# Moving the triangle of the decays from GpSimd to VectorE, with other pauses in the mixers and x loaded one tile ahead

## The chip, the cores and the metric

The kernel runs on one core of a Trainium2 chip. The metric is the device time of one launch in microseconds (us), median of three runs. One layer of a streaming encoder is computed for a prompt of 512 frames and a sample of 64.

The engines go by the names of the profile: PE is TensorE's matrix products and PEld its weight loads, DVE is VectorE, ACT is ScalarE, POOL is GpSimd, and SP issues most of the transfers. L187 is line 187 of the kernel before; the changed kernel's lines around the mixers are 2 higher.

## The reference

```python
def trunk(...):
    mod = jax.nn.silu(c) @ w_ada[l] + b_ada[l]
    sh1, sc1, g1, sh2, sc2, g2 = jnp.split(mod[:, None, :], N_MOD, axis=-1)
    h = rmsnorm(x, norm1[l]) * (1 + sc1) + sh1
    mix, s_a, s_b, s_c = token_mixers(h, ...)      # h @ w_in, mixers, @ w_out
    x = x + g1 * mix
    h = rmsnorm(x, norm2[l]) * (1 + sc2) + sh2
    f, s_f = conv_ffn(h, ...)                      # w_up, conv, silu * val, w_down
    x = x + g2 * f
    y = rmsnorm(x, final_norm)

def gdn_step(s, blk):                              # 8 heads, blocks of 64 frames
    q, k, v, g, beta = blk
    big_g = jnp.cumsum(g[..., 0], axis=-1)
    decay = jnp.exp(jnp.where(causal, big_g[..., :, None] - big_g[..., None, :], -jnp.inf))
    lower = jnp.where(strict, einsum('bhid,bhjd->bhij', kb, k) * decay, 0.0)
    sol = solve_triangular(eye + lower, concat([v * beta, kb * exp(big_g)]), unit_diagonal=True)
    u = sol[..., :dv] - einsum('bhik,bhkv->bhiv', sol[..., dv:], s)
    attn = einsum('bhid,bhjd->bhij', q, k) * decay
    o = einsum('bhid,bhdv->bhiv', q * exp(big_g), s) + einsum('bhij,bhjv->bhiv', attn, u)
    s_new = exp(g_last) * s + einsum('bhjd,bhjv->bhdv', k * exp(g_last - big_g), u)
```

Everything is float32. Beside the 8 heads of this delta rule (GDN) there are 4 heads of gated linear attention (GLA), with a decay for each channel. `q` and `k` of GDN are scaled to unit length, and each head's output is normed by its root mean square.

## The kernel before

**Projections.** A weight tile of 8 k-tiles of 128 x 128 is loaded, copied by ACT to a rounded high half `wh` (L629), and the rest is subtracted by DVE to a low half `wl` (L630); three buffers hold each half. A k-tile is six products on TensorE (L542 four times, L544 twice): high by high, high by low, low by high, each for two halves of 288 frames. After every k-tile `gemm` calls `tick`. The time from 150 us to about 1180 us holds w_in's projection and the first half of w_out's.

**Mixers.** `gdn` (9 jobs: 8 heads and one of the samples, which works in blocks of 64) and `gla` are generators. Each tick advances some of them to their next `yield`, so their instructions are written between the k-tiles. `rest(n)` yields n ticks. `self.later(n, f)` runs f after n ticks. The list of instructions of each engine is then made by a scheduler that goes by the order of writing, except that DVE's and ACT's mixer instructions (`jv`, `ja`, class `_Sooner`, all on line L1650 of the profile) are pulled forward by 80 places, and weight loads and splits as well. An engine then runs its list in order. A pause therefore decides where an instruction stands in its engine's list; when it runs is up to the data and to what stands ahead of it.

**A GDN job** goes through these steps, four blocks of 128 frames side by side in tiles of 128 x 512 (`m`):

1. `kF`, `qF` are transposed on TensorE (L145) and squared on ACT; `rsqrt` adds on DVE (L138) and takes the power −1/2 on POOL (L139).
2. Differences of the decays' sums are taken on DVE; POOL's two `affine_select` (L187, L188) set the upper or lower triangle to −200 or +200, so that the exponentials give 0 there. For the samples two POOL memsets (L190, L191) set corners too.
3. ACT scales `kT`, TensorE transposes it (L145, "bank<-consts,m"), ACT takes the exponential of `dl`; then come the products of k by k (L208) and of k by q (L216).
4. `inverse16` inverts the 16 x 16 blocks on the diagonal on POOL: DMA out (L342), loads as 32 lanes (L348), memset (L352), 14 steps of a product and a sum (L358, L359), a copy (L362), DMA out (L363), loads back (L367); DVE spreads the two results (L372). All of this stands on POOL's single list, with POOL's other work of other heads before or behind it.
5. Two levels on TensorE extend the inverse to 64 (L231, L237). Then four state steps, each with `w` copied by ACT (`sq`, half a tile) and used by L283, L299; the outputs `ops` are normed (`rsqrt` on four columns), transposed (L145) and put away.

**w_out and x.** Before each output tile of 8 k-tiles, `x_tile` loads one slice of x (L1117, L1118 on SP), transposes it (L145, "xr") and copies it to its place; `residual` adds the product to it (L1094). In the background DVE multiplies w_ada for the later modulations (L770), throughout the mixers' time.

## Time and profile before

| | us |
|---|---|
| median of 3 runs | 2985.03 (2980.51 to 2990.21) |
| the profiled execution | 2986.52 |
| its span | 2984.7 |
| PE busy | 2893.7 (97%) |
| DVE busy | 2098.1 (70%) |
| ACT busy | 1226.2 (41%) |
| POOL busy | 360.7 (12%) |
| mean granted clock of TensorE | 0.987 |

The span is what the profile shows between the first and the last instruction; 1.8 us of the execution's time lie around it. In a row of the timeline stand the start, the duration, the engine, the line, the operation, what is written and read, and in brackets the idle time ahead of it on its engine with what ended it. TensorE's clock is given as a share of the full speed.

### The profile page before, as it was taken

The page shows a single profiled execution, that of the slowest core. Times are in us where ns is not written, and L with a number is a line of the kernel's source. Part 1 is how long each engine was busy: PE and PEld are TensorE (multiplying, and loading weights), DVE is VectorE, ACT ScalarE, POOL GpSimd, SP SyncE. Part 2 cuts the span into 40 slices and gives each one's busy share as a digit, 9 for nine tenths or more (in the row PEclk, how much of TensorE's full clock was granted, in tenths as well). Part 3 has the DMA queues.
Part 4 walks back from the last instruction along what each step waited for, and adds up shares of the span by engine and source line. Part 5 has one row for each costly group of instructions (what it writes and reads, how often), then busy time and mean ns, then how long its engine had stood idle before and what let it go on. Part 6 is the DMA issues. An engine that isn't in the chain of part 4 may idle for free.

```text
span 2984.7 us, 52378 instructions
## 1 busy us (share of the span) xinstructions
PE 2893.7 (97%) x21128; PEld 2788.1 (93%) x21128; DVE 2098.1 (70%) x3225; ACT 1226.2 (41%) x2116; POOL 360.7 (12%) x634
## 2 busy tenths in 40 slices
PE   7998989999999999999999999999999999999998
PEld 3588989999889998999999999999999999999997
DVE  5776767766569877367888888888888865555555
ACT  6564544544244333255444444444444432212223
POOL 0025433234311001000000000000000000000000
PEclk9999999999999999999999999999999999999999
DMA  7855545554445547443333333333333473333221
GB/s 271 284 165 140 150 132 150 155 143 137 137 125 148 147 136 208 131 129 93 106 104 110 97 107 106 111 97 104 108 110 98 130 236 97 117 102 109 87 85 66
DMA packets 509446, 392.96 MB, mean 132 GB/s; under 512 B 41385, under 2 KB 438404, under 8 KB 509204
## 3 DMA queue, kind: packets, MB, share of 16 engines
q1 hardware_dynamic: 503780, 378.93, 42.8%
q0 software_dynamic: 5424, 10.68, 1.1%
q8 instruction: 167, 2.74, 0.4%
q14 instruction: 75, 0.61, 0.1%
HBM read 355.16 MB, written 34.36 MB: 131 GB/s over the span
## 4 chain that ended last, share of the span: by engine, by line
PE 63%; DVE 2%; DMA 1%; ACT 1%; issue 1%; POOL 0%; SPq 0%; ACTq 0%; POOLq 0%; DVEq 0%
PE g L542 19%; PE g L544 9%; PE g L1324 8%; PE g L1325 8%; PE g L1326 8%; PE bank L1324 3%; PE bank L1325 3%; PE bank L1326 3%; DVE acc L770 1%; PE bank L417 1%; DVE m L1650 0%; DVE wl L630 0%; PE bank L145 0%; PE bank L1534 0%; PE bank L776 0%
## 5 line engine op out<-in xcount | busy, mean ns | idle before, releaser
L542 PE MATMUL g<-slot,wh 128*128 128x288 f32 x3168 | 550.7, 295 | 0.2 <-DVE slot L1094 0.2
L1324 PE MATMUL g<-slot,wh 128*128 128x290 f32 x1760 | 534.0, 303 | 2.0 <-ACT p L1336 1.6
L1325 PE MATMUL g<-slot,wh 128*128 128x290 f32 x1760 | 526.8, 299 | 0.0
L1326 PE MATMUL g<-slot,wl 128*128 128x290 f32 x1760 | 521.1, 296 | 0.0
L629 ACT ACTIVATE wh<-raw 128x1024 fp32r<-128x1024 f32 x223 | 235.9, 1058 | 630.7 <-PE g L542 607.1
L542 PEld LDWEIGHTS g<-slot,wh 128*128 128x128 f32 x3168 | 463.5, 188 | 0.8 <-DVE slot L1094 0.5
L542 PE MATMUL g<-hh,wh 128*128 128x288 f32 x1984 | 458.3, 311 | 1.6 <-DVE gcb L933 1.0
L542 PE MATMUL g<-hl,wh 128*128 128x288 f32 x1984 | 437.4, 300 | 0.5 <-DVE hl L1104 0.5
L544 PE MATMUL g<-hh,wl 128*128 128x288 f32 x1984 | 434.6, 299 | 0.6 <-DVE wl L630 0.6
L1094 DVE SCALAR_TENSOR_TENSOR slot<-g,mod,slot 128x512 f32<-128x512 f32 (+1 forms) x448 | 201.8, 492 | 303.6 <-PE g L544 302.4
L1271 ACT ACTIVATE wh<-raw 128x1024 fp32r<-128x1024 f32 x176 | 186.8, 1061 | 392.6 <-PE g L1325 379.4
L1324 PEld LDWEIGHTS g<-slot,wh 128*128 128x128 f32 x1760 | 331.5, 188 | 16.5 <-ACT p L1336 10.6
L544 PE MATMUL g<-slot,wl 128*128 128x288 f32 x1584 | 341.8, 295 | 0.0
L1326 PEld LDWEIGHTS g<-slot,wl 128*128 128x128 f32 x1760 | 337.0, 191 | 0.0
L1325 PEld LDWEIGHTS g<-slot,wh 128*128 128x128 f32 x1760 | 335.6, 191 | 0.1
L542 PEld LDWEIGHTS g<-hh,wh 128*128 128x128 f32 x1984 | 320.1, 191 | 6.0 <-issue 1.4
L542 PEld LDWEIGHTS g<-hl,wh 128*128 128x128 f32 x1984 | 324.2, 191 | 1.5 <-DVE hl L1104 1.0
L630 DVE TENSOR_TENSOR wl<-raw,wh 128x1024 fp32r<-128x1024 f32 x223 | 272.5, 1222 | 73.8 <-ACT wh L629 71.1
L544 PEld LDWEIGHTS g<-hh,wl 128*128 128x128 f32 x1984 | 322.8, 190 | 1.1 <-DVE wl L630 0.8
L544 PEld LDWEIGHTS g<-slot,wl 128*128 128x128 f32 x1584 | 255.7, 188 | 0.0
L770 DVE SCALAR_TENSOR_TENSOR acc<-xr,ct,acc 128x512 f32<-128x512 f32 x322 | 229.9, 755 | 3.4 <-DMA xr<-in_w_ada_dram 3.4
L1272 DVE TENSOR_TENSOR wl<-raw,wh 128x1024 fp32r<-128x1024 f32 x176 | 214.9, 1221 | 18.6 <-ACT wh L1271 18.5
(373 smaller groups left out, 4571.0 us busy)
## 6 DMA issues: line engine op xcount, KB each, us to landing
raw<-in_w_up_dram SPq DMA_DIRECT2D x176, 512.0 KB
raw<-in_w_in_dram SPq DMA_DIRECT2D x108, 512.0 KB
raw<-in_w_down_dram SPq DMA_DIRECT2D x88, 512.0 KB
xr<-in_w_ada_dram SPq DMA_DIRECT2D x86, 512.0 KB
hraw<-in_w_ada_dram SPq DMA_DIRECT2D x64, 512.0 KB
ax<-in_w_ada_dram SPq DMA_DIRECT2D x42, 512.0 KB
raw<-in_w_out_dram SPq DMA_DIRECT2D x32, 512.0 KB
slot<-actd SPq DMA_DIRECT2D x44, 288.0 KB
```

Of the source, the lines that this page charges most:

```text
L417: T.matmul(ps[:, b * 64:(b + 1) * 64], e3[:, b], qc[:, b * 64:(b + 1) * 64], start=True, stop=True)
L542: T.matmul(ps[:, h if bank is None else bank, :n], wh, x[:, h, :n], start=f, stop=False)
L544: T.matmul(ps[:, h if bank is None else bank, :n], wl, ah[:, h, :n], start=False, stop=stop)
L629: nc.scalar.activation(hi[:, :n_], raw[:, :n_], AF.Copy)
L630: nc.vector.tensor_tensor(lo[:, :n_], raw[:, :n_], hi[:, :n_].bitcast(F32), op=ALU.subtract)
L770: V.scalar_tensor_tensor(acc[s], w[:, k], col, acc[s], op0=ALU.mult, op1=ALU.add)
L1094: self.nc.vector.scalar_tensor_tensor(x1[:, :, z], ps[:, :, c], gain[:, q:q + 1], x1[:, :, z], op0=ALU.mult, op1=ALU.add)
L1271: self.nc.scalar.activation(hi, src, AF.Copy)
L1272: self.nc.vector.tensor_tensor(lo, src, hi.bitcast(F32), op=ALU.subtract)
L1324: T.matmul(ps, wh[:, j], hi, start=(c < 3 and j == 0), stop=False, skip_group_check=True)
L1325: T.matmul(ps, wh[:, j], lo, start=False, stop=False, skip_group_check=True)
L1326: T.matmul(ps, wl[:, j], hi, start=False, stop=(j == NPAIR - 1), skip_group_check=True)
```

## The change

- A new constant `far` (128 more columns of constants) holds 200 above the diagonal and 0 elsewhere. On DVE one instruction takes the minimum of `dl` and `far` − 200, another the maximum of `dl` and `far`; POOL's two `affine_select` of each job are gone. The two memsets of the samples stay on POOL. One of five `sq` buffers makes room.
- The pause ahead of the memsets and of `kT` is REST_L = 9 instead of REST_T = 6, and stands behind the triangle.
- Each of the 14 steps of the inverse is followed by 2 ticks (1 or 2 before), REST_P is 2 for 6, 2 ticks come between the copy and the DMA, and REST_X is 12 for 16.
- REST_G, the pause of GLA's levels, is 4 for 3; `turn`, the transposes of GLA's `v`, is put off by 8 ticks instead of 3.
- x's slice is loaded while the output tile before is worked on, and transposed behind its own tile's products.

```diff
--- before.py
+++ after.py
@@ -32,10 +32,11 @@
 JOB_RATE, ADA_RATE = 1.0, 0.65
 
 
-REST_D, REST_X, REST_T, REST_N, REST_G = 8, 16, 6, 8, 3
+REST_D, REST_X, REST_T, REST_N, REST_G = 8, 12, 6, 8, 4
 REST_C = 14
-HOP, REST_P, REST_S = 3, 6, 4
+HOP, REST_P, REST_S = 3, 2, 4
 PUT, PUT_O = 24, 6
+REST_L = 9
 MOST = 2
 FAR = 200.0
 LATE = 3
@@ -77,6 +78,7 @@
     for s in LEVELS:
         m[f"p{s}"] = _pair_mask(s)
     m["bd16"] = (r[:, None] // 16 == r[None, :] // 16) * 1.0
+    m["far"] = up * FAR
     m["tri"] = up * 1.0
     m["tri2"] = (up & bd) * 1.0
     m["l127"] = np.repeat((r == 127)[:, None], P, 1) * 1.0
@@ -130,7 +132,7 @@
         return self.sp.tile([P, w], F32, tag=f"s{w}", bufs=6, name=self.name(f"s{w}"))
 
     def half(self):
-        return self.sp.tile([P, P], F32, tag="sq", bufs=5, name=self.name("sq"))
+        return self.sp.tile([P, P], F32, tag="sq", bufs=4, name=self.name("sq"))
 
 
     def rsqrt(self, out, src, n, parts=P):
@@ -183,9 +185,9 @@
         self.rsqrt(rr, ss, 8)
         dl, du = self.m4(), self.m4()
         V.tensor_tensor(dl, gb, self.col4(gcol), op=ALU.subtract)
-        yield from self.rest(REST_T)
-        nc.gpsimd.affine_select(du, dl, pattern=[[0, 4], [1, P]], compare_op=ALU.is_ge, fill=-FAR, base=0, channel_multiplier=-1)
-        nc.gpsimd.affine_select(dl, dl, pattern=[[0, 4], [-1, P]], compare_op=ALU.is_gt, fill=FAR, base=0, channel_multiplier=1)
+        V.scalar_tensor_tensor(du, self.bc4(c["far"]), -FAR, dl, op0=ALU.add, op1=ALU.min)
+        V.tensor_tensor(dl, dl, self.bc4(c["far"]), op=ALU.max)
+        yield from self.rest(REST_L)
         if pair:
             nc.gpsimd.memset(du[0:64, :, 64:P], -FAR)
             nc.gpsimd.memset(dl[64:P, :, 0:64], FAR)
@@ -351,8 +353,7 @@
             self.ja.activation(kT[:, b], kT[:, b], AF.Copy, scale=wk[:, b:b + 1])
         G.memset(lane[:, 0, 0:256:17], 1.0)
         for i in range(1, 15):
-            if i % 2:
-                yield WAIT
+            yield WAIT
             rest = slice(i + 1, 16)
             sh = [32, 15 - i, i]
             G.tensor_tensor(xt[:, rest, :i], xx[:, rest, i:i + 1].to_broadcast(sh), xx[:, i:i + 1, :i].to_broadcast(sh), op=ALU.mult)
@@ -360,6 +361,7 @@
             yield WAIT
         yield from self.rest(REST_P)
         G.tensor_copy(xt, xx.rearrange("p i j -> p j i"))
+        yield from self.rest(2)
         G.dma_start(d1.rearrange("w q f -> q w f"), lane)
         yield from self.rest(REST_S)
         cm = self.sp.tile([P, 2, 4, 16], F32, tag="cm", bufs=2, name=self.name("cm"))
@@ -1074,7 +1076,7 @@
                     if f == 1:
                         x["v"] = lambda: [vT[b // 2][:, b % 2] for b in range(4)]
 
-                self.later(HOP, turn)
+                self.later(REST_T + 2, turn)
             if h == 3:
                 xs["v"] = self.gla_sample_v
             for f in range(2):
@@ -1108,14 +1110,18 @@
         return lambda k0, k1: (self.i[name][0, (k_off + k0) * P:(k_off + k1) * P, m * P:(m + 1) * P]
                                .rearrange("(k p) n -> p k n", p=P))
 
-    def x_tile(self, m):
-
-        nc, i = self.nc, self.i
-        t = self.slot(self.x_place(m), F32)
-        raw = self.xr()
+    def x_load(self, m):
+
+        nc, i, raw = self.nc, self.i, self.xr()
         n = slice(m * P, (m + 1) * P)
         nc.sync.dma_start(raw[:, :512].rearrange("p (b t) -> p b t", b=4), i["x_prompt"][0, :, n].rearrange("(b p) n -> p b n", p=P))
         nc.sync.dma_start(raw[:TS, 512:512 + P], i["x_sample"][0, :, n])
+        return raw
+
+    def x_tile(self, m, raw):
+
+        nc = self.nc
+        t = self.slot(self.x_place(m), F32)
         nc.gpsimd.memset(t[:, :, HP:ZS], 0.0)
         ps = self.transpose4(raw[:, :512].rearrange("p (b t) -> p b t", b=4))
         nc.scalar.activation(t[:, :, :HP], ps.rearrange("p (h b) t -> p h (b t)", h=2), AF.Copy)
@@ -1599,10 +1605,13 @@
                     K.run_later(all=True)
                     ob = [K.load_o(k, lambda k=k: K.htiles(k)) for k in range(8, 16)]
                     K.x1 = []
+                    raw = K.x_load(0)
                     for m in range(KD):
                         ps = K.pgt()
-                        K.x1.append(K.x_tile(m))
                         K.gemm(ps, K.w_cols("w_out", m, 8), ob, tick=K.tick)
+                        nxt = K.x_load(m + 1) if m + 1 < KD else None
+                        K.x1.append(K.x_tile(m, raw))
+                        raw = nxt
                         K.residual(ps, K.x1[m], K.mod[:, 2, m])
                     K.drain()
                     for _ in K.ada:
```

How the order of the instructions moves is shown at three places. The first is ACT's list where head 4's differences (m_727 and m_728 before, m_734 and m_735 now) stand near head 2's first `w` (sq_676), the copy that TensorE's L283 reads. Before:

```order
L1650 ACT_TABLE_LOAD
L1650 ACTIVATE m_711_4474<-m_711_4474 128x512
L1650 ACTIVATE m_647_4042<-bank_673_4294,beta_1586 128x128 x4
L1650 ACTIVATE m_727_4625<-m_727_4625 128x512
L1650 ACTIVATE m_728_4626<-m_728_4626 128x512
L1650 ACTIVATE sq_676_4331<-bank_675_4329 128x128
L1650 ACTIVATE m_727_4625<-m_727_4625,nbeta_1608 128x128 x3
L1650 ACTIVATE m_647_4042<-bank_679_4344,rq_466_2817 128x128
```

And in the change:

```order
L1659 ACTIVATE m_644_4023<-bank_674_4283,beta_1586 128x128 x4
L1659 ACT_TABLE_LOAD
L1659 ACTIVATE m_711_4452<-m_711_4452 128x512
L1659 ACTIVATE sq_676_4318<-bank_675_4316 128x128
L1659 ACTIVATE m_734_4633<-m_734_4633 128x512
L1659 ACTIVATE m_735_4634<-m_735_4634 128x512
L1659 ACTIVATE m_644_4023<-bank_679_4330,rq_463_2792 128x128
L1659 ACTIVATE m_734_4633<-m_734_4633,nbeta_1608 128x128 x4
```

Head 2's `w` stands ahead of head 4's two exponentials instead of behind them; the table load ahead of them is there in both.

The second is POOL's list at the end of inverse 7 (L363 and L367 before, L365 and L369 now), where the samples' memsets (m_1171 and m_1170 before, m_1177 and m_1176 now) follow. Before:

```order
L363 DMA d1_1082_7258<-m_1042_6913 32x2x256
L367 DMA cm_1178_7908<-d1_1082_7258 128x4x16 x2
L187 AFFINE_SELECT m_1171_7868<-m_1170_7867 128x512
L188 AFFINE_SELECT m_1170_7867<-m_1170_7867 128x512
L190 MEMSET m_1171_7868 64x4x64
L191 MEMSET m_1170_7867 64x4x64
L303 DMA out_3_dram<-st_1150_7696 128x128
L139 TENSOR_TENSOR s8_1153_7703<-s8_1153_7703,mhalf_93 128x4
L946 DMA od14_77<-m_962_6374 256x1x256
L139 TENSOR_TENSOR s8_1164_7827<-s8_1164_7827,mhalf_93 128x8
```

And in the change:

```order
L365 DMA d1_1088_7277<-m_1043_6896 32x2x256
L369 DMA cm_1186_7956<-d1_1088_7277 128x4x16 x2
L192 MEMSET m_1177_7857 64x4x64
L193 MEMSET m_1176_7856 64x4x64
L305 DMA out_3_dram<-st_1150_7673 128x128
L141 TENSOR_TENSOR s8_1153_7680<-s8_1153_7680,mhalf_93 128x4
L948 DMA od14_77<-m_969_6392 256x1x256
L141 TENSOR_TENSOR s8_1165_7806<-s8_1165_7806,mhalf_93 128x8
```

The two selects have left this list; the memsets and the two roots stand where they stood.

The third is SP's list at the first slices of x (xr_1879 and xr_1889 before, xr_1874 and xr_1884 now) among w_out's weights. Before:

```order
L628 DMA raw_1909_12644<-in_w_out_dram 128x8x128
L628 DMA raw_1918_12725<-in_w_out_dram 128x8x128
L917 DMA sd_ar1_89<-ts_1852_12337 128x64
L1117 DMA xr_1879_12390<-in_x_prompt_dram 128x4x128
L1118 DMA xr_1879_12390<-in_x_sample_dram 64x128
L785 DMA xr_1886_12456<-in_w_ada_dram 128x2x512
L923 DMA qkv_1885_12423<-sd_ar1_89 128x256
L1117 DMA xr_1889_12477<-in_x_prompt_dram 128x4x128
L1118 DMA xr_1889_12477<-in_x_sample_dram 64x128
L628 DMA raw_1926_12796<-in_w_out_dram 128x8x128
```

And in the change:

```order
L630 DMA raw_1906_12597<-in_w_out_dram 128x8x128
L1117 DMA xr_1874_12337<-in_x_prompt_dram 128x4x128
L1118 DMA xr_1874_12337<-in_x_sample_dram 64x128
L630 DMA raw_1915_12678<-in_w_out_dram 128x8x128
L787 DMA xr_1883_12409<-in_w_ada_dram 128x2x512
L630 DMA raw_1923_12749<-in_w_out_dram 128x8x128
L919 DMA sd_ar1_89<-ts_1849_12284 128x64
L925 DMA qkv_1882_12396<-sd_ar1_89 128x256
L1117 DMA xr_1884_12426<-in_x_prompt_dram 128x4x128
L1118 DMA xr_1884_12426<-in_x_sample_dram 64x128
L787 DMA xr_1892_12475<-in_w_ada_dram 128x2x512
```

The first slice's load stands one of w_out's weight tiles earlier than before, and the second slice's two tiles behind the first's instead of next to it.

## The prediction

> **What bounds the kernel now.** I read the page's busy table first, then busy time by stretch (stretch, length, PE, PEld, DVE, ACT, POOL, granted clock, DMA share, GB/s), then TensorE's waits by releaser (total us, times, longest).
>
> ```profile
> PE 2893.7 (97%) x21128; PEld 2788.1 (93%) x21128; DVE 2098.1 (70%) x3225; ACT 1226.2 (41%) x2116; POOL 360.7 (12%) x634
> 150.00:1180.00 1030.00, 975.93 (x7322) 946.27 (x7319) 737.05 (x1286) 454.00 (x1086) 275.64 (x461) 0.98 0.52 147
> 1400.00:2985.00 1585.00, 1571.64 (x11619) 1554.67 (x11617) 1142.39 (x1575) 588.47 (x719) 71.92 (x137) 1.00 0.36 109
> PE bank L145 <- ACT m L1650: 23.3, 6, 9.9
> PE bank L283 <- ACT sq L1650: 12.1, 3, 6.6
> PE bank L417 <- DVE m L1650: 4.6, 4, 2.5
> PE bank L145 <- DMA xr<-in_x_prompt_dram: 3.5, 2, 2.7
> ```
>
> TensorE sets the end: 97% busy, and nothing is idle for long behind 1400 us. All edits lie in 150 to 1180 us, where mixers run between the k-tiles of the projection. There TensorE is idle for 1030 − 976 = 54 us and has clock 0.98. The only thing to win is those idle 54 us and the clock lost behind them; TensorE's own work is unchanged. So I price each stall by the instruction that ended last before it.
>
> **The affine_selects.** POOL runs its queue in order, and head 3's inverse stands there ahead of head 4's affine_selects. Timeline (start, duration, work, idle before and its releaser):
>
> ```profile
> 414.27 1.56 POOL L367 DMA_DIRECT2D cm<-d  x2 [1.67 <-DMA d<-m]
> 417.23 1.15 ACT L1650 ACTIVATE m<-m 128x512 f32<-128x512 f32 x2 [6.88 <-POOL m L188]
> 418.29 0.26 ACT L1650 ACTIVATE sq<-bank 128x128 f32<-128x128 f32 x1
> 418.60 0.80 PE L283 MATMUL bank<-sq,m 128*128 128x128 f32 x2 [6.58 <-ACT sq L1650]
> 491.66 0.49 PE L283 MATMUL bank<-sq,m 128*128 128x128 f32 x2 [1.35 <-ACT sq L1650]
> 705.83 0.31 POOL L191 MEMSET m<- 64x256 f32 x1
> 707.02 0.49 PE L283 MATMUL bank<-sq,m 128*128 128x128 f32 x2 [4.14 <-ACT sq L1650]
> ```
>
> Stretches behind four gaps, columns as above:
>
> ```profile
> 418.60:428.60 10.00, 10.00 (x57) 10.00 (x58) 3.10 (x7) 4.92 (x13) 0.00 (x0) 0.69 0.04 8
> 491.70:501.70 10.00, 10.00 (x57) 10.00 (x58) 4.92 (x11) 3.55 (x9) 0.00 (x0) 0.66 0.18 54
> 707.00:717.00 10.00, 9.98 (x65) 9.64 (x66) 5.25 (x11) 6.71 (x19) 0.00 (x0) 0.83 0.30 77
> 992.10:1002.10 10.00, 9.96 (x79) 9.99 (x80) 6.61 (x16) 4.50 (x9) 0.00 (x0) 1.00 0.23 61
> ```
>
> The inverse's last DMA issue ends at 415.83, then come the two selects, ACT's exponentials of head 4 follow, and behind them, in ACT's order, the copy `w` (`sq`) of head 2 that TensorE waits for. On DVE the triangle is finished long before, so the 6.58 us go, and with them the clock of the next 10 us, 10 × (1 − 0.69) = 3.1: **−9.7**. The stall at 490 has the same chain: 1.35 + 3.4 = **−4.7**. At 703 it is different: this is the sample job, and its two memsets stay on POOL behind inverse 7. Only the 1.3 us of selects go (0.63 each, by a row below), and in the order the place where `w` is needed comes 0.7 k-tile sooner (32 before, 31.3 now): 0.6 us of that gain are lost, and inverse 7 may run slower. I take **−0.5**, between 0 and 4.14 + 1.7 = 5.8.
>
> Here, one rule to weigh against the clock column. The Trainium skill (TensorE: Matmul & The Clock Gate, "HAM oscillation — how this bites in real kernels") has the clock fall only where TensorE is idle for more than about 3.4 us. The trace agrees with the gap at 418 and not with that at 491, where 1.35 us went with 0.66; the 2.51 us ahead of 992 went with 1.00. By the rule the clock terms at 490, 880, 1165 and 194 (7.7 us in all) would stay away, and the estimate would be 2968.
>
> **The other stalls.** What follows comes from pauses counted in k-tiles. One is 0.9 us long: from head 0's products at 202.98 to TensorE's arrival at 237.33 − 9.89 = 227.44 the order has 27.2 k-tiles.
>
> ```profile
> 194.56 2.03 POOL L139 TENSOR_TENSOR s<-s,mhalf 128x8 f32<-128x8 f32 x1 [4.09 <-DVE s L138]
> 197.05 0.48 PE L145 MATMUL bank<-consts,m 128*128 128x128 f32 x1 [3.26 <-ACT m L1650]
> 202.98 1.05 PE L208 MATMUL bank<-m 128*128 128x128 f32 x8
> 220.10 0.63 POOL L188 TENSOR_SCALAR_AFFINE_SELECT m<-m 128x512 f32<-128x512 f32 x1
> 235.18 1.70 POOL L139 TENSOR_TENSOR s<-s,mhalf 128x8 f32<-128x8 f32 x1
> 237.33 0.99 PE L145 MATMUL bank<-consts,m 128*128 128x128 f32 x3 [9.89 <-ACT m L1650]
> 779.03 0.56 POOL L303 DMA_DIRECT2D out_dram<-st  x1
> 781.54 1.04 POOL L139 TENSOR_TENSOR s<-s,mhalf 128x4 f32<-128x4 f32 x1 [1.95 <-DVE s L138]
> 783.07 0.47 PE L145 MATMUL bank<-consts,m 128*128 128x128 f32 x1 [6.82 <-ACT m L1650]
> 882.78 0.48 PE L145 MATMUL bank<-consts,qkv 128*128 128x128 f32 x1 [2.90 <-ACT qkv L1067]
> 1160.47 0.39 SPq L1117 DMA_DIRECT2D xr<-in_x_prompt_dram  x1
> ```
>
> And the stretches behind three of these gaps:
>
> ```profile
> 197.10:207.10 10.00, 10.00 (x59) 10.00 (x60) 7.29 (x12) 6.95 (x16) 0.77 (x1) 0.71 0.42 141
> 882.80:892.80 10.00, 10.00 (x70) 9.86 (x71) 8.52 (x24) 6.09 (x12) 0.00 (x0) 0.86 0.04 10
> 1165.10:1175.10 10.00, 9.88 (x61) 9.12 (x62) 5.06 (x8) 2.48 (x5) 2.84 (x4) 0.83 0.85 250
> ```
>
> - At 194 TensorE waits for head 0's root on POOL. REST_L is 3 above the REST_T it replaces, but only 1.7 k-tiles of work now stand in between more (62.3 to 64.0). 1.6 us of the gap go and 0.4 of the clock's 2.9: **−2.8**.
> - At 227 head 1's root stands on POOL behind the whole inverse of head 0, as it still does. From head 0's products (202.98) to 237.33 are 34.3 us. Head 1's two selects, 1.3 us, leave that queue: 33.0. TensorE arrives after 29 k-tiles in place of 27.2, 1.7 us later: the gap of 9.89 becomes 6.9, **−3.0**. The inverse's steps standing 2 k-tiles apart cost POOL nothing by themselves: it runs by data. The pauses in it sum to 43 k-tiles before (21 + 6 + 16) and 44 now (28 + 2 + 2 + 12), so what is done behind it comes no later on that account.
> - At 776 the root of head 7's output waits for its DVE add, which stood behind the two L372 products that wait for inverse 8. Now the add stands ahead, and POOL can go on when its DMA issue at 779.03 ends (779.6, not 781.5): **−1.9**. POOL's inverse 8 is still ahead.
> - At 880 the transposes of `v` wait for ACT; `turn` is put 8 k-tiles off rather than 3, and stands 3 k-tiles later in the order. 1.0 of 2.9 may remain, since another product now comes ahead: −1.9, with the clock 1.4: **−3.3**.
> - GLA: REST_G is 1 more, the levels stand 0.7 k-tile later; of four waits of 4.6 us together about half go: **−2.4**.
> - x: the load is issued at 1160.47 and awaited until 1165.1. Now it is issued one output tile, 8 k-tiles or 7 us, ahead of its use. 3.5 + 1.7 of clock go; the PSUM tile now becomes free only behind the transposes and their copy, for which I set 1.0: **−4.2**.
> - Against this, roots of three outputs now stand 0.7 (head 2) and 4.1 k-tiles (head 5: 2.7 in place of 6.8) closer behind their last product, head 6 2.2 further. The chain from product to transpose took at least 3.1 us at head 6 (716.59 to 719.73), and 2.7 k-tiles are 2.4 us: **+1.5** over the three.
>
> ```profile
> 716.59 0.39 PE L299 MATMUL bank<-st,qkv 128*128 128x128 f32 x2
> 719.73 0.33 PE L145 MATMUL bank<-consts,m 128*128 128x128 f32 x1 [1.02 <-ACT m L1650]
> ```
>
> - `sq` with 4 buffers for 5: a copy `w` (0.26 us at 418.29) may have to wait for TensorE to have read an older one. Over 4 steps of 9 jobs that is 9 us at most; with two live per step and the steps a k-tile apart, I take nothing.
>
> Sum of these: −9.7 −4.7 −0.5 −2.8 −3.0 −1.9 −3.3 −2.4 −4.2 +1.5 = **−31.0**.
>
> **What it adds.**
>
> ```profile
> L770 DVE SCALAR_TENSOR_TENSOR acc<-xr,ct,acc 128x512 f32<-128x512 f32 x322 | 229.9, 755 | 3.4 <-DMA xr<-in_w_ada_dram 3.4
> L1650 DVE TENSOR_TENSOR m<-m,cum 128x512 f32<-128x512 f32 x9 | 6.1, 680 | 0.7 <-DMA m<-gd 0.7
> L1650 ACT ACT_TABLE_LOAD x22 | 28.2, 1283 | 1.4 <-DVE m L1650 1.0
> PE bank L713 <- DVE wl L630: 2.7, 5, 0.8
> 471.60:483.40 11.80, 11.80 (x95) 11.63 (x94) 4.74 (x7) 4.28 (x10) 9.61 (x29) 1.00 0.41 125
> 676.20:696.80 20.60, 20.60 (x167) 20.14 (x166) 19.53 (x31) 6.51 (x13) 18.40 (x29) 1.00 0.72 207
> ```
>
> DVE gets 9 three-operand and 9 two-operand instructions on 128x512: 9 × (0.755 + 0.680) = 12.9 us. They lie beside TensorE's work as DVE's other 737 us do; DVE is idle for 293 of the 1030 us. If that cover were gone, all 12.9 would be paid. TensorE waited on DVE's weight split for some 2.7 us in five places, so DVE is rarely the last: I take **+2**. In the order ACT gets 8 more table loads, 8 × 1.283 = 10.3 us, between copies that TensorE sometimes waits for; ACT is 44% busy there: bounds 0 and 10.3, taken **+2**. POOL's 28 steps took 11.8 us with DVE 40% busy (4.74 of 11.80), 20.6 with DVE 95% busy. The added DVE work can lengthen an inverse that TensorE waits for (heads 0, 7, 8) by 1.43 us at most each, 0 to 4.3 in all: **+1**.
>
> Net: −31 + 5 = −26. The profiled execution took 2986.5 (span 2984.7, 1.8 around it), 1.5 above the median: 2986.5 − 26 = **2960**. The bounds of costs and of 703 make its own range 2948 to 2975.
>
> **Rivals.** *Little is gained.* The waits move rather than go: inverse 7, inverse 8 and inverse 0 still stand ahead of memsets and roots, and the copy `w` at 412 then waits for the next late thing on ACT. For it: POOL's order, apart from the selects, is the same; the steps slow by 20.6/11.8 beside a busy DVE. Against it: at 412 and 490 no other late instruction is seen. Half of 412 and 490 (7.2), all of x (4.2), the small ones −5, cost 5 to 10: about −8, **2979**. The Trainium skill (GPSIMD Engine Reference, "1. Specifications") says that GpSimd shares its SBUF interfaces with VectorE, with contention where a DVE instruction has two SBUF inputs; the added ones are of that sort, and the two step rows agree.
>
> *All stalls go.* If 703 (5.3 more), 227 (6.9) and 776 (4.9) are gone with everything else, about −17 more: **2943**. For it: more k-tiles stand between; against: POOL's queue still holds them.
>
> *Slower.* The triangle is pulled ahead of weight splits on DVE, and TensorE waits for the low half of the weights: 1.43 us at each of nine jobs, each with a clock loss as at 418 (3.1): 9 × 4.5 = 41 against −31, **2997**. It decides once a split comes within 1.43 us of its first product. Against it: the low half is split up to two weight tiles (14 us) ahead and the trace shows few such waits.
>
> **The numbers.** Forecast 0.52, little 0.21, all 0.13, slower 0.14. A measurement here can tell 0.3%, 9 us: faster is below 2976. The forecast and "all" lie there, with a small part of "little" and less a part of the forecast's edge: faster 0.66, same 0.21, slower 0.13. The range goes from just under "all" (2941) over "little" to no change (2985), leaving out the slower case and tails.
>
> **What would show it.** Right: no 6.58 us wait ahead of head 2's L283 near 412 and 490, and clock about 1.00 behind; 227 and 776 shorter but present, 703 nearly as long; x's wait gone; TensorE idle near 54 − 20 = 34 us in the stretch up to w_out's end. Wrong: new waits on the split of weights, or on ACT behind a table load, or TensorE waiting as long at 227, 703 and 776 while 412 and 490 go elsewhere.

## The result, and the profile after

The changed kernel takes 2975.81 us in the median of 8 runs (2968.78 to 2980.01), the kernel before 2985.53 (2980.51 to 2997.09, 8 runs). The ratio is 0.9958, with a 95% interval of 0.9942 to 0.9974: 10 us faster by the medians, where 25 were forecast. The time lies inside the stated range of 2941 to 2985, but the gain is 0.4 of the forecast's. The profiled execution took 2975.75 us, its span is 2974.0.

TensorE's share and its waits in the changed kernel (total us, times, longest; lines 2 higher than before):

```profile
PE 2892.8 (97%) x21128; PEld 2786.1 (94%) x21128; DVE 2106.4 (71%) x3243; ACT 1232.6 (41%) x2124; POOL 359.1 (12%) x616
PE bank L147 <- ACT m L1659: 19.2, 8, 9.8
PE bank L285 <- ACT sq L1659: 9.9, 1, 9.9
PE bank L419 <- DVE m L1659: 5.0, 4, 2.6
PE bank L147 <- DMA xr<-in_x_prompt_dram: 2.1, 2, 1.8
```

Three waits of L283 (L285 now) had summed to 12.1 us; two of them are gone, and the one that is left has 9.9 by itself. The next two blocks show where that happened: the same stretches of the kernel before, then of the changed one (stretch, length, PE, PEld, DVE, ACT, POOL, granted clock, DMA share, GB/s). What TensorE loses in a stretch is its length less PE's busy time, and roughly the length times the missing clock.

```profile
150.00:222.00 72.00, 65.28 (x471) 63.08 (x469) 53.53 (x107) 43.38 (x101) 14.03 (x22) 0.95 0.60 168
222.00:260.00 38.00, 27.69 (x201) 26.99 (x201) 25.20 (x39) 15.24 (x43) 17.28 (x31) 0.87 0.51 141
400.00:520.00 120.00, 110.81 (x821) 108.46 (x820) 75.55 (x126) 58.29 (x162) 37.65 (x76) 0.93 0.44 125
650.00:735.00 85.00, 79.84 (x612) 78.53 (x612) 48.26 (x78) 39.03 (x112) 33.52 (x48) 0.98 0.48 139
735.00:850.00 115.00, 108.02 (x827) 104.30 (x826) 70.94 (x111) 30.15 (x70) 26.69 (x45) 0.97 0.50 144
850.00:1180.00 330.00, 316.16 (x2303) 301.34 (x2302) 257.89 (x497) 136.98 (x252) 33.82 (x62) 0.99 0.51 148
```

```profile
150.00:222.00 72.00, 67.28 (x489) 63.14 (x488) 59.40 (x118) 51.28 (x121) 10.51 (x15) 1.00 0.62 174
222.00:260.00 38.00, 28.20 (x188) 27.75 (x187) 21.30 (x33) 10.85 (x27) 16.84 (x33) 0.82 0.51 146
400.00:520.00 120.00, 117.43 (x910) 114.36 (x909) 88.56 (x146) 60.95 (x173) 42.99 (x78) 1.00 0.50 142
650.00:735.00 85.00, 74.21 (x563) 72.44 (x562) 45.88 (x75) 34.63 (x90) 32.21 (x45) 0.94 0.42 121
735.00:850.00 115.00, 112.56 (x858) 108.27 (x857) 71.28 (x113) 32.26 (x74) 26.10 (x45) 0.99 0.53 151
850.00:1180.00 330.00, 321.34 (x2358) 309.22 (x2357) 262.11 (x504) 140.84 (x256) 34.32 (x62) 0.99 0.53 153
```

Idle time and clock together: 150 to 222 gains 2.0 + 3.6; 222 to 260 loses 1.4 (0.5 less idle, 1.9 more clock); 400 to 520 gains 6.6 + 8.4; **650 to 735 loses 5.6 + 3.4**; 735 to 850 gains 4.5 + 2.3; 850 to 1180 gains 5.2. These six come to 22 us of gain. Against them stand the head, up to 150 us, whose code is the same and which was some 3.5 us longer in this execution (below), 0.8 us more of idle time in each of the stretches from 260 to 400 and from 520 to 650, and some 3 us from 1180 to 1500 (2.0 of idle time, 0.9 of clock), where some short waits grew (the longest, of L1330 for ACT, from 1.6 to 2.4 us). That leaves 14 us where the two spans differ by 10.7: some 3 us are not placed, and a clock of two digits does not place them.

The stretch that got worse holds the end of inverse 7, the samples' corner fills behind it and head 6's copy `w` behind those. Some rows of POOL and ACT there, in the kernel before (the fills' last row and the product are with the prediction):

```profile
668.42 0.62 POOL L342 DMA_DIRECT2D d<-m  x1 [10.28 <-DVE m L1650]
706.17 0.63 ACT L1650 ACTIVATE m<-m 128x512 f32<-128x512 f32 x1 [4.86 <-POOL m L191]
706.71 0.26 ACT L1650 ACTIVATE sq<-bank 128x128 f32<-128x128 f32 x1
```

And POOL, ACT and PE in the changed kernel, without two short rows of ACT:

```profile
665.72 0.61 POOL L344 DMA_DIRECT2D d<-m  x1 [13.86 <-DVE m L1659]
704.18 0.31 POOL L193 MEMSET m<- 64x256 f32 x1
704.16 0.63 ACT L1659 ACTIVATE m<-m 128x512 f32<-128x512 f32 x1 [9.87 <-POOL m L192]
704.81 1.28 ACT L983 ACT_TABLE_LOAD   x1
706.10 0.60 ACT L983 ACTIVATE gt<-g 128x512 f32<-128x512 f32 x1
706.95 1.07 ACT L631 ACTIVATE wh<-raw 128x1024 fp32r<-128x1024 f32 x1
707.89 0.29 ACT L1659 ACTIVATE sq<-bank 128x128 f32<-128x128 f32 x1
708.23 0.80 PE L285 MATMUL bank<-sq,m 128*128 128x128 f32 x2 [9.86 <-ACT sq L1659]
```

The wait went from 4.14 to 9.86 us, and its 5.7 us more divide in three. From the inverse's first DMA issue to the end of the fills were 37.7 us before (668.42 to 706.14) and are 38.8 now (665.72 to 704.49), though the two selects, 1.3 us, have left: +1.05. TensorE reached the product 34.5 us behind that issue (707.02 − 4.14 = 702.88) and now 32.65 (708.23 − 9.86 = 698.37): it comes earlier and so waits longer, +1.8. And between the fills' end and the product ACT now has a table load, a silu and a weight copy to do ahead of `w`: 0.9 us before, 3.7 now, +2.9.

### The profile page after: what moved, and what is told of

It reads as the page before. It is cut to its first block, busy times and chain, and to the rows that moved or that the text cites. A ratio compares the mean times of both kernels' runs of the same rounds, so it can differ in the third digit from the quotient of the medians.

```text
span 2974.0 us, 52340 instructions
## 1 busy us (share of the span) xinstructions
PE 2892.8 (97%) x21128; PEld 2786.1 (94%) x21128; DVE 2106.4 (71%) x3243; ACT 1232.6 (41%) x2124; POOL 359.1 (12%) x616
## 3 DMA queue, kind: packets, MB, share of 16 engines
q1 hardware_dynamic: 503780, 379.00, 42.8%
## 4 chain that ended last, share of the span: by engine, by line
PE 86%; DVE 4%; POOL 3%; DMA 2%; issue 2%; ACT 2%; ACTq 0%; SPq 0%; POOLq 0%; DVEq 0%
PE g L544 29%; PE g L546 14%; PE g L1330 8%; PE g L1331 8%; PE g L1332 8%; PE bank L1331 3%; PE bank L1330 3%; PE bank L1332 3%; PE bank L147 1%; DVE acc L772 1%; PE bank L778 1%; POOL m L359 1%; PE bank L419 1%; POOL m L360 1%; PE bank L710 1%
## 5 line engine op out<-in xcount | busy, mean ns | idle before, releaser
L1330 PE MATMUL g<-slot,wh 128*128 128x290 f32 x1760 | 533.4, 303 | 2.6 <-ACT p L1342 2.6
L631 ACT ACTIVATE wh<-raw 128x1024 fp32r<-128x1024 f32 x223 | 236.1, 1059 | 673.4 <-PE g L544 651.9
L1330 PEld LDWEIGHTS g<-slot,wh 128*128 128x128 f32 x1760 | 331.2, 188 | 16.8 <-ACT p L1342 11.6
```

The source lines that it names most:

```text
L631: nc.scalar.activation(hi[:, :n_], raw[:, :n_], AF.Copy)
L1330: T.matmul(ps, wh[:, j], hi, start=(c < 3 and j == 0), stop=False, skip_group_check=True)
```

## The experiments

Each kernel ran beside the kernel before on its chip; the last column is the difference of the two medians. The ratio is not the quotient of these medians, and the two measures differ by up to 2.8 us (most for the change, which is 12.5 us faster by the ratio), so a few us between two kernels of the table decide nothing.

| kernel | median us | ratio to before, 95% | us against before |
|---|---|---|---|
| the change | 2975.8 | 0.9958 (0.9942 to 0.9974) | −9.7 |
| e2: triangle alone | 2971.0 | 0.9965 (0.9952 to 0.9978) | −11.6 |
| e3: all but the triangle | 2992.0 | 1.0038 (1.0024 to 1.0051) | +9.5 |
| e12: change, REST_L = 6 | 2962.1 | 0.9931 (0.9916 to 0.9946) | −20.3 |
| e5: change, inverse's pauses back | 2972.2 | 0.9968 (0.9953 to 0.9983) | −11.4 |
| e4: change, x back | 2970.7 | 0.9957 (0.9942 to 0.9972) | −12.8 |
| e6: change, triangle twice | 2972.4 | 0.9964 (0.9949 to 0.9979) | −11.1 |
| e1: change, corner fills on VectorE | 2959.9 | 0.9926 (0.9912 to 0.9941) | −22.6 |
| e8: change, roots on ScalarE | 2956.9 | 0.9919 (0.9903 to 0.9936) | −25.7 |
| e9: e1 and e8 together | 2946.8 | 0.9872 (0.9855 to 0.9890) | −36.7 |
| e11: e9 with the old pauses and x | 2960.2 | 0.9927 (0.9913 to 0.9942) | −22.2 |
| e10: e9, all roots, REST_G = 5 | 2942.6 | 0.9869 (0.9853 to 0.9886) | −39.8 |
| e13: e10 with REST_L = 6 | 2943.5 | 0.9864 (0.9848 to 0.9881) | −39.4 |

The expectations call the copy at 700 us head 7's; it is head 6's, since head 7's inverse is the one that has just ended. Three parts of the change were not tried by themselves: GLA's REST_G, the delay of `v`, and the fifth `sq` buffer, which goes and comes with the triangle in e2 and e3.

### e1: the corner fills off GpSimd's list

```diff
-            nc.gpsimd.memset(du[0:64, :, 64:P], -FAR)
-            nc.gpsimd.memset(dl[64:P, :, 0:64], FAR)
+            V.memset(du[0:64, :, 64:P], -FAR)
+            V.memset(dl[64:P, :, 0:64], FAR)
```

> The changed kernel, with the two corner fills of the sample job done by VectorE instead of GpSimd. Theory A (what is left of the loss is GpSimd's list: the fills stand behind inverse 7, ScalarE's exponential waits for them, and head 7's copy w stands behind it): the 9.86 us wait of L285 near 700 us goes with the 10.2 us of half clock behind it, 9.9 + 5.1 = 15 us less than the changed kernel's 2975.8, so near 2961, ratio to the kernel before near 0.991. Rival B (the wait is made by ScalarE's own list, where a table load, a silu and a weight copy now stand between the exponential and w, 2.9 us): only what is above 2.9 us of it moves, to another late instruction, and the gain is 0 to 5 us, ratio 0.994 to 0.996. Rival C (VectorE, now with the triangle, is the late one): no gain.

2959.91 us, 22.6 under the kernel before. Its head (for the last section) and the stretch of the wait:

```profile
0.00:150.00 150.00, 128.03 (x580) 72.77 (x581) 97.33 (x156) 88.67 (x138) 5.66 (x16) 0.97 0.84 278
650.00:735.00 85.00, 84.15 (x656) 82.32 (x656) 59.57 (x98) 35.67 (x91) 34.26 (x47) 1.00 0.54 151
```

From 650 to 735 us TensorE is idle for 0.85 us in place of 10.8, with full clock: 13 us over the change by the differences to before and 9.5 by the ratios, where theory A had 15. Inverse 7 ran for 41.7 us here, 3.6 longer than in the change, and `w` did not wait. So the wait is made by GpSimd's list and what hangs behind it on ScalarE's.

### e8: the roots off GpSimd's list

```diff
-        self.rsqrt(rr, ss, 8)                    # DVE adds EPS, POOL takes the power -1/2
+        V.tensor_scalar_add(rr, ss, EPS)
+        A.activation(rr, rr, AF.Ln)
+        A.activation(rr, rr, AF.Exp, scale=-0.5)
```

> The changed kernel with the root of the eight sums of squares of q and k taken by ScalarE (exponential of minus half the logarithm) instead of GpSimd's power. Theory A (at 227 TensorE waits for head 1's root, which stands on GpSimd behind the whole inverse of head 0): the 9.8 us wait goes with 13.7 us of half clock (6.9), and some 25 more table loads of 1.28 us on ScalarE cost some 3 us: 13 us less than the changed kernel, ratio near 0.9915. Rival B (the squares or the transposes are late themselves): a wait of 5 us or more of L147 on ScalarE stays at the same place; ratio near 0.995. Rival C: the table loads make ScalarE late elsewhere and eat the gain, ratio 0.996 or more without the wait at 227.

Unlike the addition that it replaces, e8's stands among VectorE's mixer instructions, which are pulled forward; in the change the root waited for GpSimd alone (no idle time ahead of it at 236.75, below).

2956.87 us, 25.7 under before, 16 more than the change (11.6 by the ratios). The stretch around head 1's transposes:

```profile
222.00:260.00 38.00, 38.00 (x296) 37.87 (x294) 28.75 (x45) 21.30 (x40) 23.62 (x41) 1.00 0.56 168
```

No idle time is left there, so theory A holds at 227; the 25 more table loads (77 for 52) left the gain standing. The wait at 700 us, now 10.2 us long, is untouched.

### e9: both

e9 has the edits of e1 and of e8.

> The changed kernel with both repairs: the samples' corner fills on VectorE and the eight-column roots on ScalarE. Theory A (two separate waits on GpSimd's list): the gains add, 15.0 + 19 us less than the changed kernel, near 2942, ratio 0.986 to 0.987, no wait of 5 us or more left between 165 and 1385 us. Rival B (they share a cause, or the table loads on ScalarE meet the exponentials of the samples): at least 8 us of it missing, ratio 0.989 or more.

2946.83 us. Over the change the single gains were 12.9 and 16.0 by the differences to before, and both together give 27.0: they add, as theory A said. It had 34, from single gains of 15 and 19, and its ratio of 0.986 to 0.987 is just missed (0.9872). The longest wait between 165 and 1385 us is 2.6 us.

### e2: the triangle alone

The kernel before, with the constant, the two VectorE instructions, four `sq` buffers, and all else as it was.

```diff
+        V.scalar_tensor_tensor(du, self.bc4(c["far"]), -FAR, dl, op0=ALU.add, op1=ALU.min)
+        V.tensor_tensor(dl, dl, self.bc4(c["far"]), op=ALU.max)
         yield from self.rest(REST_T)
-        nc.gpsimd.affine_select(du, dl, ...)
-        nc.gpsimd.affine_select(dl, dl, ...)
```

> The kernel before with the triangle on VectorE alone (with its constant and one sq buffer less); pauses and x loads as before. Theory A: the waits at 412 and 490 go with their clock (9.7 + 4.7), the one at 703 loses about 1 us, those at 194, 227, 776, 880 and of x stay: 14 us less, ratio near 0.9953. Rival B (the pauses gave a gain of the triangle back): 20 to 26 us less, ratio 0.991 to 0.993. Rival C (the triangle costs on VectorE what it saves): within 5 us, ratio 0.998 or more.

2970.95 us, 11.6 under before where theory A had 14. The waits at 412 and 490 are gone, that near 700 is 3.5 us, those near 194, 227, 762 and 866 are within 0.8 us of what they were: theory A in every place. **One edit alone gives what the whole change gives, within the noise.** The others must cost, somewhere, what they win elsewhere.

### e3: all but the triangle

```diff
-        V.scalar_tensor_tensor(du, self.bc4(c["far"]), -FAR, dl, op0=ALU.add, op1=ALU.min)
-        V.tensor_tensor(dl, dl, self.bc4(c["far"]), op=ALU.max)
         yield from self.rest(REST_L)
+        nc.gpsimd.affine_select(du, dl, ...)
+        nc.gpsimd.affine_select(dl, dl, ...)
```

> The changed kernel with the triangle back on GpSimd (affine_select, five sq buffers); pauses and x loads as changed. Theory A: 412 and 490 are back in some form, the gains at 194, 776, 880 and of x (5.4 + 6.1 + 4.6 + 3.4 = 19.5) are kept, the wait near 700 us is at least as long as in the changed kernel (9 us more than before): about 8 us less than before, ratio 0.996 to 0.999. Rival B (the pauses lose): not faster than before, ratio 1.000 or more. Rival C (the pauses alone are the whole gain): ratio 0.9958 as with the whole change.

2992.0 us: 9.5 slower than before, so rival B. Its waits of L283 (L284 here), which were 12.1 us in three before:

```profile
PE bank L284 <- ACT sq L1658: 24.3, 4, 11.9
```

They are at 414 (3.9), 489 (3.0), 635 (5.6) and 710 (11.9). The new pauses lengthen the very kind of wait that the triangle removes. Between e3 and the whole change lies the triangle alone, worth 19 us here where it is worth 11.6 with the old pauses.

### e5: the inverse's pauses back

```diff
         for i in range(1, 15):
-            yield WAIT
+            if i % 2:
+                yield WAIT
...
-        yield from self.rest(2)                  # ahead of the DMA; REST_P 2 -> 6, REST_X 12 -> 16
```

> The changed kernel with the pauses of the inverse as before (steps 1 or 2 ticks apart, REST_P 6, REST_X 16, no 2 ticks ahead of the DMA); triangle, REST_L, REST_G, x and v as changed. On ScalarE's list the samples' exponentials now stand behind head 7's second copy w and next to the third, without the table load, silu and weight copy in between. Theory A' (the wait near 700 grew because of the place of the exponential on ScalarE's list, which the inverse's pauses moved; its steps themselves run by data and are not slower or faster): the wait falls from 9.9 to 2 to 5 us with half of its clock, 227 stays at about 9.9: 5 to 9 us less than the changed kernel, ratio 0.992 to 0.9945. Rival B (the spaced steps matter because GpSimd then runs slower or faster): the inverse from its first DMA issue to its last changes by more than 3 us in the mean. Rival C (these pauses do nothing): ratio 0.9958.

2972.17 us, ratio 0.9968, the change's within the intervals: these pauses do nothing that can be measured, rival C. Theory A' missed: `w` is ahead of the samples' exponentials now and only the next copy stands behind, and still TensorE waits for 7.1 us at 696, because inverse 7 took 42.8 us (38.1 in the change). So the place on ScalarE's list is not the whole of it, and the spacing of the steps is not what makes the inverse long.

### e12: REST_L as before

```diff
-REST_L = 9
+REST_L = 6
```

> The changed kernel with REST_L = 6, as the pause before. On ScalarE's list the samples' two exponentials then stand ahead of head 7's w with only one short instruction between, without the table load, silu and weight copy. Theory A' (the place of that exponential on ScalarE's list made the wait near 700 grow from 4.1 to 9.9): the wait is 3 to 6 us there, and the one near 194 is back at about 3.3 with half clock behind it: within 4 us of the changed kernel, ratio 0.9945 to 0.997. Rival B (the wait near 700 grew by the inverse's longer run): it stays at 8 us or more.

2962.07 us, 20.3 under before, more than theory A' allowed. The wait near 700 is not 3 to 6 us, it is gone:

```profile
685.09 0.31 POOL L193 MEMSET m<- 64x256 f32 x1 [0.64 <-DVE m L1659]
686.98 0.26 ACT L1659 ACTIVATE sq<-bank 128x128 f32<-128x128 f32 x1
687.29 0.49 PE L285 MATMUL bank<-sq,m 128*128 128x128 f32 x2
```

The fills end 33.5 us behind the inverse's first issue at 651.9, and the product comes 35.4 us behind it and does not wait. REST_L changes ScalarE's list and the inverse's length at once, so e12 does not divide the wait between the two. The wait near 194 is back (2.97), as expected, and the one at 754 is 4.7. What differs is seen in the stretches of inverses 6 and 7 themselves (from first to last DMA issue), before, in the change, and in e12:

```profile
601.10:630.30 29.20, 29.20 (x237) 28.74 (x237) 20.59 (x34) 7.53 (x16) 19.20 (x38) 1.00 0.47 125
668.40:704.20 35.80, 34.48 (x277) 33.78 (x275) 31.56 (x49) 10.73 (x22) 25.34 (x39) 1.00 0.62 175
```

```profile
596.30:633.60 37.30, 37.28 (x296) 36.27 (x295) 31.63 (x51) 15.19 (x35) 26.24 (x38) 1.00 0.50 139
665.70:703.80 38.10, 32.67 (x259) 31.75 (x257) 30.59 (x50) 9.30 (x18) 25.74 (x39) 0.97 0.58 165
```

```profile
584.70:614.00 29.30, 29.30 (x238) 28.84 (x237) 20.69 (x34) 7.53 (x16) 19.46 (x38) 1.00 0.44 125
651.90:684.00 32.10, 32.10 (x259) 31.63 (x259) 28.51 (x44) 9.09 (x20) 21.43 (x38) 1.00 0.61 177
```

The length of inverses 4 to 7 goes with REST_L. Their mean is 29.0 us before, 29.0 in e2, 27.9 in e12 and 27.4 in e13, all with a pause of 6; it is 33.9 in the change, 33.6 in e3, 34.4 in e5, 33.7 in e6 and 33.5 in e10, all with 9. The other inverses do not follow it: 0 to 3 take 34.3 us in the mean before and 33.2 in the change, and inverse 8 is the shorter one with the longer pause (31.7 us against 34.2). At inverse 6 VectorE is busier with the longer pause (31.6 us in 37.3 against 20.6 in 29.2). At inverse 7, the one that the fills stand behind, it is not: 31.6 us in 35.8 before, 30.6 in 38.1 in the change, 28.5 in 32.1 in e12. So why that one got longer stays open. That the pause moves an inverse beside other VectorE work, and that this slows GpSimd, fits inverse 6 and was not tried by itself.

### e4 and e6: x, and the cover of VectorE

e4 loads and transposes x ahead of its own tile again:

```diff
+                        K.x1.append(K.x_tile(m))
                         K.gemm(ps, K.w_cols("w_out", m, 8), ob, tick=K.tick)
-                        nxt = K.x_load(m + 1) if m + 1 < KD else None
-                        K.x1.append(K.x_tile(m, raw))
```

> The changed kernel with x loaded and transposed ahead of its own output tile, as before. Theory A: the two waits for x's load, 3.5 us, and one clock loss of 1.7 come back in place of the 2.1 us that the changed kernel still waits: 1 to 4 us more, ratio 0.996 to 0.9975. Rival B (the move is worth all of the forecast's 4.2 or more): 5 us more or above. Rival C (it costs, by the PSUM tile that is held longer): faster than the changed kernel.

Ratio 0.9957 against 0.9958: moving x is worth nothing that can be measured, and theory A's 1 to 4 us can't be told from it. e4 waits 3.8 us for x, the change 2.1.

e6 does the two triangle instructions a second time, with the same result:

```diff
+        V.scalar_tensor_tensor(du, self.bc4(c["far"]), -FAR, du, op0=ALU.add, op1=ALU.min)
+        V.tensor_tensor(dl, dl, self.bc4(c["far"]), op=ALU.max)
```

> The changed kernel with the triangle's two VectorE instructions done twice in each of the nine jobs (the second pair changes nothing in the values): 18 more instructions, 12.9 us of VectorE's time. Theory A (they are covered): 0 to 3 us more, ratio 0.9955 to 0.997. Rival B (VectorE's added work is what the gain went into): 8 us more or above, ratio 0.9985 or more, with more waits of TensorE on VectorE or a longer inverse.

Ratio 0.9964 against 0.9958, the intervals nearly the same: VectorE's added work is covered, theory A. The inverses 4 to 7 are no longer in the mean than in the change (33.7 us), and in e2, which has these instructions with the old pause, they are as before, so these instructions are not what slowed them.

### e11, e10, e13: what the pauses are worth once GpSimd's list is free

e11 is e2 with the edits of e1 and e8; e10 is e9 with the four-column roots on ScalarE too and REST_G = 5; e13 is e10 with REST_L = 6.

> The kernel before with the triangle and the samples' corner fills on VectorE and the eight-column roots on ScalarE; pauses, v and x as before. Theory D (the pauses were needed only for what stood on GpSimd's list; once that is off the list they are worth only the waits at 880, 776 and of the next transposes): 4 to 12 us more than with both repairs on the changed kernel (2946.8, ratio 0.9872), so ratio 0.9885 to 0.9915, with waits near 776 (6.7) and 880 (2.9) left and none near 227 and 700. Rival E (the pauses themselves carry much): ratio 0.993 or more. Rival F (the pauses cost): ratio 0.987 or less.

2960.15 us, ratio 0.9927, just above theory D's 0.9885 to 0.9915 and short of rival E. The waits that D named are there: 6.8 us at 748, 2.9 at 853, none near 227 or 700; waits of 2.4 us at 278 and 1.9 at 341 are new. The new pauses and x together are worth 14 us once the two repairs are in (e11 to e9), 2 us with the triangle alone (e2 to the change, against them, within the noise), and they cost 9.5 with neither (e3).

> The changed kernel with both repairs, the four-column roots on ScalarE too, and REST_G = 5 for 4. Theory A: the wait near 748 (2.4 us) goes with its 1.7 us of clock, GLA's two waits of 2.6 and 1.8 us shrink by 0.9 each, and the short waits of 0.9 to 1.6 us of the other heads' outputs shrink by some tenths; 18 or more table loads on ScalarE cost 2 us: 4 to 8 us less than with both repairs (2946.8), ratio 0.9845 to 0.986. Rival B (ScalarE's table loads, 95 in place of 77, make as much): ratio 0.9865 to 0.988. Rival C: ScalarE becomes late, ratio 0.989 or more.

2942.62 us, ratio 0.9869 to e9's 0.9872: no difference that can be measured, rival B's range. What theory A wanted to shrink hardly did: the wait at 748 is still 2.1 us, GLA's two are 2.6 and 1.5.

> The kernel with both repairs, the four-column roots on ScalarE and REST_G = 5 (2942.6, ratio 0.9869), with REST_L = 6 for 9. Theory G (REST_L = 9 costs only by the wait near 700, that is by the longer inverses 4 to 7 and the earlier product behind the samples' fills; with the fills off GpSimd's list it costs nothing): within 5 us, ratio 0.985 to 0.9885, while inverses 4 to 7 fall from 33.5 us to 28 us in the mean, and the wait near 194 is 1 to 2 us longer. Rival H (the longer inverses cost by themselves, in places that are not seen as single waits): 6 us less or more, ratio 0.9848 or below. Rival I (REST_L = 9 is needed): 6 us more, ratio 0.989 or above.

2943.51 us, ratio 0.9864: theory G. Inverses 4 to 7 are 27.4 us in the mean in place of 33.5, and the time is the same; only the wait near 194 is not longer, as it was said to be, but 1.4 us in both. So the long inverses cost only where something waits behind them on a list. e10 and e13 are the best of these kernels, 1.3% faster than the kernel before.

## Why the prediction was right or wrong

**Right.** TensorE's stalls were the place to look, and the selects at 412 and 490 were priced rightly: e2, with them alone, has 11.6 us, and in the change the stretch from 400 to 520 gained 15.0 where 14.4 was forecast. The cost on VectorE was rightly put near nothing: the instructions take 6.5 + 6.2 us (forecast 12.9), and doubling them moves nothing that can be measured.

```profile
L1659 DVE SCALAR_TENSOR_TENSOR m<-consts,m 128x512 f32<-128x512 f32 x9 | 6.5, 726 | 0.9 <-PE bank L253 0.8
L1659 DVE TENSOR_TENSOR m<-m,consts 128x512 f32<-128x512 f32 x9 | 6.2, 684 | 0.1
```

The root of head 7's output went ahead of VectorE's spreading, as said: POOL goes on right behind its issue. The wait is 2.4 us where 4.9 was forecast, and that is luck: inverse 8 was 2.5 us shorter, which the prediction had not said. With REST_L = 6 (e12) inverse 8 is as long as before and the wait 4.7 us. Changed kernel:

```profile
777.34 0.56 POOL L305 DMA_DIRECT2D out_dram<-st  x1
777.91 1.06 POOL L141 TENSOR_TENSOR s<-s,mhalf 128x4 f32<-128x4 f32 x1
779.45 0.33 PE L147 MATMUL bank<-consts,m 128*128 128x128 f32 x1 [2.39 <-ACT m L1659]
```

The wait at 194 fell by 2.0 us and with it all of its half clock (5.6 in the stretch, −2.8 forecast), and that at 880 for `v` fell from 2.9 to 0.3.

**Wrong: the term of the samples' fills at 703, "I take −0.5, between 0 and 4.14 + 1.7 = 5.8" of gain.** It is a loss of 9.0, 5.7 of waiting and 3.4 of clock, and the bounds left out a loss. The prediction had seen that the fills stay behind inverse 7 and that `w` is needed 0.7 k-tile sooner, 0.6 us; TensorE came 1.8 us sooner. It had said that inverse 7 may run slower, but allowed 1.43 us at most, for the triangle's own work on VectorE; with the new pauses the inverse became 2.4 us longer. And it put ScalarE's list at nothing without a reason: the exponential that waits for the fills got a table load, a silu and a weight copy between itself and `w`, 2.9 us, which the list in the order of the changed kernel could have shown. All three go back with REST_L: e12, which changes only that pause, is 10.6 us better than the change by the differences to before (8 by the ratios), and e1, which moves the fills, 12.9 (9.5). Either way the time comes to about the forecast's, by different waits than it names, so that is no support for its sum.

**Wrong: the wait of head 1's root at 227, −3.0.** It stayed (9.80), with 1.9 us more of clock loss in its stretch:

```profile
236.75 1.70 POOL L141 TENSOR_TENSOR s<-s,mhalf 128x8 f32<-128x8 f32 x1
238.90 1.25 PE L147 MATMUL bank<-consts,m 128*128 128x128 f32 x4 [9.80 <-ACT m L1659]
```

From the inverse's first DMA issue (205.14 before, 206.01 now) to the root's end are 31.7 and 32.4 us: the selects' 1.3 us left POOL's list, and the way through the two DMA trips and the steps took 2 us more. TensorE came 0.8 us later, not 1.7, so nothing was left. Why the two trips and the steps took longer is open. e8 shows that the mechanism was right: off the list, the wait is gone.

**Smaller misses.** GLA, −2.4: four waits of 5.0 us for 4.6, nothing gained. Outputs' roots, +1.5: the short waits of L147 behind heads 2 to 6 and one new wait of L253 make some 3.5 us more than before. x, −4.2: no gain by e4. The load was to be issued 7 us ahead of its use; the third slice's was issued 3.7 us ahead, and the second's 3.1:

```profile
1165.79 0.37 SPq L1117 DMA_DIRECT2D xr<-in_x_prompt_dram  x1
1169.46 0.63 PE L147 MATMUL bank<-consts,xr 128*128 128x128 f32 x4 [1.79 <-DMA xr<-in_x_prompt_dram]
```

**The sum and the signs.** The prediction's own range, 2948 to 2975, does not follow from its bounds: with the costs at 0, and at 12.9 + 10.3 + 4.3, in place of the 5 taken, and 703 between 0 and 5.8, it is some 2950 to 2983. Its signs of being wrong came in part: 227 waited as long as before and 703 longer, and TensorE was idle for 42 us from 150 to 1180 where 34 was named, for 54 before.

**The rivals.** "Little is gained" (2979) named what happened: the waits behind GpSimd's list move rather than go. It had no price for a wait that grows. "All stalls go" (2943) needs the two repairs (e9, 2946.8). "Slower" by late weight splits did not come even with the added work doubled (e6).

**The clock.** By the Trainium skill's rule (TensorE: Matmul & The Clock Gate, "HAM oscillation — how this bites in real kernels") TensorE should have no idle gaps above about 3.4 us. The runs agree for the long gap at 229, 9.8 us, with a clock of 0.57 behind it. As a limit below which gaps cost nothing it does not hold: behind the 2.4 us at 777 the clock was 0.83, behind the 2.6 us at 881 it was 1.00:

```profile
238.90:248.90 10.00, 10.00 (x49) 9.77 (x50) 5.37 (x10) 6.05 (x15) 0.00 (x0) 0.57 0.65 190
779.50:789.50 10.00, 10.00 (x65) 9.98 (x66) 2.52 (x3) 3.12 (x7) 0.71 (x1) 0.83 0.27 78
883.40:893.40 10.00, 9.88 (x78) 9.71 (x78) 9.33 (x25) 5.45 (x9) 0.00 (x0) 1.00 0.21 57
```

## What to carry to other kernels

Work on an engine that runs its list in order is priced by what stands ahead of it there; moving half of a chain off such a list (the selects) leaves the other half (fills, roots) behind the same blocker, so look through the list for all of them. A pause that shifts one job against another can also change how long another job's steps take and what stands on a third engine's list, as REST_L did here: a term at such a place needs a bound on the side of loss. Measure pauses with and without the edit that they come with, since here the same pauses, with x, cost 9.5 us, gave nothing that can be measured, or gained 14 us, by what else was on GpSimd's list.

## What the runs showed that was not expected

The head, up to 150 us, is the same code in the change and in e1. Its clock was 0.93 in the change's profile and 0.97 in e1's (shown there), as in the kernel before: the narrow projection behind it (first product of L829) began at 153.1 and at 149.5 us. The changed kernel's head:

```profile
0.00:150.00 150.00, 128.14 (x564) 72.95 (x565) 94.97 (x152) 86.73 (x134) 5.65 (x16) 0.93 0.82 272
```

TensorE's busy time is nearly the same in both (128.1 and 128.0 us). So 3.6 us of a single execution here go with the clock and not with the code, and the trace of one execution can't place the last few us of a difference of 10. GpSimd's inverse of 28 small steps took from 23.5 us (e13, head 5) to 42.8 us (e5, head 7) from first to last DMA issue, for the same work.
